# One stored value instead of a high and a low part for the mixers' results

## The chip, the cores and the metric

The kernel runs on one core of a Trainium2 chip. The metric is the device time of one launch in microseconds (us), the median of several runs. One execution was recorded by the hardware profiler. TensorE (PE) multiplies matrices and loads weights (PEld); VectorE (DVE), ScalarE (ACT) and GpSimd (POOL) work on tiles in on-chip memory (SBUF) and on PE's accumulators (PSUM banks). Each of them carries out its own instructions strictly in order. DMA transfers move data between DRAM and SBUF; they are issued by SyncE's queue (SP) or by POOL's.

## The reference: one hybrid layer

1152 tokens (1024 of a new stream, 8 times 16 of running streams) go through one layer of width 1024, all float32. What the change touches is the seam between the three mixers and the output projection:

```
xa, ga, z, xbc, dt, q, fpre, ig, og = split(rmsnorm(x) @ w_in)
ya = rglru(causal_conv(xa)) * gelu(ga)        # mixer A, 256 columns
yb = ssd_mixer(z, xbc, dt)                    # mixer B, 512 columns
yc = hgrn_mixer(q, fpre, ig, og)              # mixer C, 256 columns
x  = x + concat(ya, yb, yc) @ w_out           # output projection
x  = x + ffn(rmsnorm(x))                      # SwiGLU, then a last rmsnorm
```

## The kernel before

**Numbers.** Each float32 operand of a large product is split into a high part of type fp32r and a low part, the remainder. One product is then three matmuls, high·high, high·low and low·high (`mm3`, lines 142 to 147). A split is an ACT copy that rounds (line 180) and a subtraction (line 181), on DVE or POOL.

**Tiles.** The tokens are 9 tiles of 128, in 3 chunks of 3 tiles (384 tokens). Activations are held transposed: 128 channels on the partitions, tokens along the free axis. A chunk of the mixers' results is 8 blocks of 128 channels: blocks 0 and 1 come from mixer A, 2 to 5 from mixer B, 6 and 7 from mixer C.

**Stages.** First norm; input projections; mixer C for each token tile (`mix_c`, line 495); mixer A for each of its two channel blocks, all tokens at once (`mix_a`, line 350); the projections for B (`proj_xbc`, `proj_z`); then chunk by chunk mixer B for each tile (`mix_b`, line 686), the chunk's load (`mixt`, line 802) and the output projection with residual (`w_out`, line 812); then the feed-forward part, from about 600 us to the end.

**The buffer in DRAM.** `mixd` (line 111) holds the high and the low part of each value. `mix_a` makes them in two tiles `yh` and `yl` (line 391; the subtraction is POOL's) and issues 8 writes per block on SP. `mix_c` makes them from PSUM in the tile `mo`, with two ACT copies (line 631) and two DVE subtractions (line 632) per token tile, and issues two writes. `mix_b` does likewise in one of its work tiles (`ws` or `wb`, line 795) for the first two token tiles of a chunk; the third is split straight into the chunk's tile `mT` (line 793). `mixt` loads a chunk from `mixd` into `mT` with six transfers on POOL's queue: four of 2 blocks (384 KB) and two of 4 blocks for two token tiles (512 KB), all high parts and low parts alternating by blocks.

**Where mT lies.** `slot` (line 227) gives `mT` of chunk 0 the place of the last chunk's normed input, `mT` of chunk 1 the place that holds `s0f`, mixer B's states of the 8 running streams, which must first be computed and written out, and `mT` of chunk 2 the place of `ws`, mixer B's second set of work tiles.

**Order.** A scheduler in the framework places instructions per engine by priorities and by its own model of time. `feed()` (line 150) raises the priority of weight loads, their splits and evictions by 3000; `mix_b` is raised by 2000. `S` tiles (line 345 on: `rawxa`, `xa`, `g`, `yh`, ...) share six buffers of 128x1152 float32. `pw` is the PSUM bank of an output projection, `xr` its result with the residual, `wr_o`, `wh_o`, `wl_o` the raw, high and low weights of it, `pmb` and `pmc` the banks in which B's and C's results are transposed.

Of the kernel before, what the change touches and what calls it, by code (L numbers as in the profile page):

```python
# [11 lines left out]
F32 = mybir.dt.float32  # L12
F32R = mybir.dt.float32r
BF16 = mybir.dt.bfloat16
U8 = mybir.dt.uint8
AF = mybir.ActivationFunctionType
ALU = mybir.AluOpType

P = 128
D = 1024  # L20
KD = 8
NCHUNK = 3
TPC = 3
CH = TPC * P
# [66 lines left out]
def hybrid_step(ctx, tc, xT, xTp, vec, rows, nrow, wch, wtk0, wtk1, wout, wgate, wup, wdown,  # L91
# [3 lines left out]
    V, S, G, T = nc.vector, nc.scalar, nc.gpsimd, nc.tensor  # L95
    dma = nc.sync.dma_start
# [6 lines left out]
    dp = ctx.enter_context(tc.tile_pool(name="dp", bufs=1, space=bass.MemoryType.DRAM))  # L103
# [4 lines left out]
    zd = dp.tile([NT, P, 512], F32, tag="zd", name="zd")  # L108
    vod = dp.tile([NT, P, 512], F32, tag="vod", name="vod")
    qkbd = dp.tile([NT, P, 8 * P], F32, tag="qkbd", name="qkbd")  # L110
    mixd = dp.tile([NCHUNK, P, 2, KD, CH], F32, tag="mixd", name="mixd")
    ad = dp.tile([72, P], F32, tag="acd", name="acd")

    p1 = tc.tile_pool(name="p1", bufs=1)
# [24 lines left out]
    def mm(out, lhsT, rhs, start=True, stop=True):  # L139
        T.matmul(out, lhsT, rhs, start=start, stop=stop)  # L140
# [8 lines left out]
    def feed():  # L149
        return tc.high_priority(offset=PRI)  # L150
# [28 lines left out]
    def split(dst_hi, dst_lo, src, eng):  # L179
        S.activation(dst_hi, src, AF.Copy)  # L180
        eng.tensor_tensor(dst_lo, src, dst_hi.bitcast(F32), ALU.subtract)  # L181

    pr = p1.__enter__()
# [5 lines left out]
    hnw = pr.tile([P, 2], F32, name="hnw")  # L189
# [37 lines left out]
    def slot(c, name, dt=F32R):  # L227
        return xp.tile([P, 2, KD, CH], dt, tag=f"hT{c}", name=name)
# [79 lines left out]
    def stile(name, dt=F32):  # L308
        return pr.tile([P, NTOK], dt, tag="S", name=name, bufs=SB)
# [40 lines left out]
    def mix_a(j):  # L350
        x = conv_tile(j, j, [vc[:, V_CWA + i * 2 + j:V_CWA + i * 2 + j + 1] for i in range(4)],
                      vc[:, V_CBA + j:V_CBA + j + 1], f"xa{j}")
        ga = plain_tile(2 + j, f"ga{j}")

        t1, t2 = stile(f"a1_{j}"), stile(f"a2_{j}")
        for g, dst in ((0, t1), (1, t2)):
            for c in range(NCHUNK):
                cs = slice(c * CH, (c + 1) * CH)
                pb = bank("a", f"pa{j}{g}{c}", [CH])
                mm(pb, wbd[:, g * 2 + j, :], x[:, cs])  # L360
                S.activation(dst[:, cs], pb, AF.Tanh, bias=hb[:, g * 2 + j:g * 2 + j + 1], scale=0.5)
        t4, t3 = stile(f"a4_{j}"), stile(f"a3_{j}")
        S.activation(t4, t1, AF.Exp, bias=sp2[:, 2 + j:3 + j], scale=sp2[:, 2 + j:3 + j])
        S.activation(t1, t1, AF.Tanh, bias=sp2[:, j:j + 1], scale=sp2[:, j:j + 1])
        V.scalar_tensor_tensor(t2, t2, 1.0, x, ALU.add, ALU.mult)
        S.activation(t4, t4, AF.Identity, bias=cst[:, 1:2], scale=0.5)
        V.scalar_tensor_tensor(t3, t1, 1.0, t4, ALU.add, ALU.mult)
        V.scalar_tensor_tensor(t3, t3, 2.0, t4, ALU.subtract, ALU.mult)
        S.activation(t1, t1, AF.Sqrt)
        V.scalar_tensor_tensor(t1, t1, -1.0, t3, ALU.mult, ALU.mult)  # L370
        G.tensor_tensor(t2, t2, t1, ALU.mult)
        S.activation(t3, t3, AF.Identity, bias=cst[:, 3:4], scale=-2.0)
        sm = pr.tile([P, NB], F32, tag="sm", name=f"sm{j}")
# [12 lines left out]
        S.activation(t4, t4, AF.Identity, bias=ones[:, 0:1], scale=0.044715)
        G.tensor_tensor(t4, t4, ga, ALU.mult)
        S.activation(t4, t4, AF.Tanh, scale=float(np.sqrt(2.0 / np.pi)))
        V.scalar_tensor_tensor(t4, t4, 1.0, ga, ALU.add, ALU.mult)
        V.scalar_tensor_tensor(t4, t4, 0.5, t1, ALU.mult, ALU.mult)  # L390
        yh, yl = stile(f"yh{j}", F32R), stile(f"yl{j}", F32R)
        split(yh, yl, t4, G)
        for hl, v in enumerate((yh, yl)):
            for p, t, n in ((0, 1, 3), (3, 0, 1), (4, 4, 2), (6, 6, 3)):
                dma(mixd[p // TPC, :, hl, j, p % TPC * P:(p % TPC + n) * P], v[:, t * P:(t + n) * P].bitcast(F32))

# [96 lines left out]
    def mix_c(t):  # L495
# [12 lines left out]
        if not samp:  # L508
# [12 lines left out]
            for i in (1, 2, 3):  # L521
                n = 32 * i
# [53 lines left out]
        for h in range(4):  # L576
            j, r = h // 2, (h % 2) * 64
# [25 lines left out]
        else:  # L603
            pn = bank("c", f"pnc_{t}", [2, 64])
            for h in range(4):
                j, r = h // 2, (h % 2) * 64
# [18 lines left out]
        pm = bank("d", f"pmc{t}", [2, P])  # L625
        for j in range(2):
            T.transpose(pm[:, j, :], of[:, j * P:(j + 1) * P], ident)
        mo = pr.tile([P, 2, 2, P], F32R, tag="mo", name=f"mo{t}")
        for j in range(2):
            hn = hnw[:, j:j + 1]  # L630
            S.activation(mo[:, 0, j], pm[:, j, :], AF.Copy, scale=hn)
            V.scalar_tensor_tensor(mo[:, 1, j], pm[:, j, :], hn, mo[:, 0, j].bitcast(F32), ALU.mult, ALU.subtract)
        c, i = POS[t] // TPC, POS[t] % TPC
        for hl in range(2):
            dma(mixd[c, :, hl, 6:8, i * P:(i + 1) * P], mo[:, hl].bitcast(F32))
        if t == NT - 1:
            dma(o_psc, Sc)

# [47 lines left out]
    def mix_b(t, last):  # L686
        samp, first = t == 0, t == 1
        c, i = POS[t] // TPC, POS[t] % TPC
        dt, da, acs, tot, ex, tl = [sml[:, j, :] for j in range(6)]
        hc = slice(t * 8, t * 8 + 8)  # L690
        cs = slice(i * P, (i + 1) * P)
        bcount[0] += 1
        if bcount[0] % 2:
            wk6 = [pr.tile([P, 1024], F32, tag="S", name=f"wb{t}_{j}", bufs=SB) for j in range(6)]
        else:
            wk6 = [st["ws"][:, j, :] for j in range(6)]
# [91 lines left out]
        pm = bank("d", f"pmb{t}", [4, P])  # L788
        for k in range(4):
            T.transpose(pm[:, k, :], yf[:, k * P:(k + 1) * P], ident)  # L790
        if last:
            mT = st["mT", c]
            split(mT[:, 0, 2:6, cs], mT[:, 1, 2:6, cs], pm, V)
        else:
            mo = wk6[5].bitcast(F32R).rearrange("p (a k s) -> p a k s", a=2, s=P)
            split(mo[:, 0], mo[:, 1], pm, V)
            for hl in range(2):
                dma(mixd[c, :, hl, 2:6, cs], mo[:, hl].bitcast(F32))
        if t == NT - 1:
            dma(o_psb, Sb)  # L800

    def mixt(c):
        mT = slot(2 - c, f"mT{c}")
        st["mT", c] = mT
        for hl in range(2):
            for ks in ((0, 2), (6, 8)):
                G.dma_start(mT[:, hl, ks[0]:ks[1], :], mixd[c, :, hl, ks[0]:ks[1], :])
        for hl in range(2):
            G.dma_start(mT[:, hl, 2:6, 0:2 * P], mixd[c, :, hl, 2:6, 0:2 * P])


    def w_out(c):
# [119 lines left out]
    for t in range(NT):  # L932
        mix_c(t)
# [531 lines left out]
```

## Time and profile before

| | |
|---|---|
| time, median of 3 runs | 1440.03 us (1437.41 to 1441.8) |
| profiled execution, device time | 1439.05 us |
| its span on the core | 1437.3 us |
| PE busy | 1362.8 us (95%) |
| DVE, ACT, POOL busy | 1048.0, 544.5, 523.1 us (73%, 38%, 36%) |
| moved by DMA | 194.78 MB, 136 GB/s |

Busy time is the sum of an engine's instructions. With PE busy for 95% of the span, another engine's work costs time only where PE waits for it, or where PE runs at its lower clock. [...] The columns "idle before" tell what released an instruction that had waited.

### The profile page before, as it was taken

How to read it: one execution, taken by the hardware profiler on the slowest of the kernel's cores; microseconds unless marked ns; L12 is line 12 of the kernel's file. 1: busy time of each engine (PE TensorE's matmuls, PEld its weight loads, DVE VectorE, ACT ScalarE, POOL GpSimd, SP SyncE). 2: the span in 40 equal slices, each digit the busy share in tenths (PEclk: the TensorE clock that was granted, in tenths of full speed). 3: DMA queues.
4: the chain of work that ended last, by engine and by line, in shares of the span. 5: the costliest groups of instructions: out<-in, count | busy, mean ns of one | idle time of the engine just before them, and what ended most of it. 6: DMA issues, size and time to landing. Idle time of an engine off the chain costs nothing.

```text
span 1437.3 us, 24425 instructions
## 1 busy us (share of the span) xinstructions
PE 1362.8 (95%) x9383; PEld 1311.7 (91%) x9383; DVE 1048.0 (73%) x1923; ACT 544.5 (38%) x969; POOL 523.1 (36%) x417
## 2 busy tenths in 40 slices
PE   8998998999999999898999999999999999999986
PEld 7898887899998798798999999999999999989985
DVE  8475588878767575699556566565676688999896
ACT  7232276344455254465323222232222453333222
POOL 4160042211014420223554454544554533452453
PEclk9999999899999899898999999999999999999998
DMA  6264032433277877851422332222323263544523
GB/s 238 71 209 133 30 94 73 110 104 114 71 229 272 263 231 259 280 173 61 140 73 74 117 107 98 79 80 105 117 88 104 98 212 107 178 138 126 167 67 132
DMA packets 107001, 194.78 MB, mean 136 GB/s; under 512 B 10812, under 2 KB 66564, under 8 KB 106756
## 3 DMA queue, kind: packets, MB, share of 16 engines
q1 hardware_dynamic: 101988, 185.35, 39.7%
q0 software_dynamic: 4896, 7.87, 1.9%
q8 instruction: 74, 1.21, 0.4%
q14 instruction: 43, 0.35, 0.1%
HBM read 136.77 MB, written 56.41 MB: 134 GB/s over the span
## 4 chain that ended last, share of the span: by engine, by line
PE 37%; DVE 13%; DMA 6%; POOL 2%; issue 2%; ACT 1%; SPq 0%; DVEq 0%; POOLq 0%; ACTq 0%
PE pS_g L145 3%; PE pS_u L145 3%; PE pS_g L147 3%; PE pS_u L146 3%; PE pS_g L146 3%; PE pS_u L147 3%; PE pA_u L147 2%; PE pA_u L145 2%; PE pA_u L146 2%; PE pA_g L146 2%; PE pA_g L145 2%; PE pA_g L147 2%; PE pd L145 2%; PE pd L146 2%; PE pd L147 2%
## 5 line engine op out<-in xcount | busy, mean ns | idle before, releaser
L145 PE MATMUL pd<-e,as 128*128 128x256 f32 (+1 forms) x560 | 168.1, 302 | 8.2 <-ACT as L180 4.0
L146 PE MATMUL pd<-e,as 128*128 128x256 f32 (+1 forms) x560 | 166.0, 297 | 0.0
L147 PE MATMUL pd<-e,as 128*128 128x256 f32 (+1 forms) x560 | 163.0, 298 | 2.7 <-DVE as L181 2.6
L145 PEld LDWEIGHTS pd<-e,as 128*128 128x128 f32 x560 | 106.7, 191 | 11.7 <-ACT as L180 5.1
L181 POOL TENSOR_TENSOR al_u<-wr_u,ah_u 128x1024 fp32r<-128x1024 f32 x30 | 72.0, 2401 | 115.5 <-ACT ah_u L180 112.6
L147 PEld LDWEIGHTS pd<-e,as 128*128 128x128 f32 x560 | 105.9, 191 | 4.5 <-DVE as L181 4.3
L146 PEld LDWEIGHTS pd<-e,as 128*128 128x128 f32 x560 | 107.0, 191 | 0.1
L181 POOL TENSOR_TENSOR al_g<-wr_g,ah_g 128x1024 fp32r<-128x1024 f32 x30 | 72.0, 2400 | 93.9 <-ACT ah_g L180 93.2
L180 ACT ACTIVATE ah_g<-wr_g 128x1024 fp32r<-128x1024 f32 x30 | 31.7, 1060 | 142.6 <-PE pS_u L146 80.5
L1071 POOL TENSOR_TENSOR g<-g,pt_u 128x256 f32<-128x256 f32 (+1 forms) x80 | 77.0, 982 | 19.7 <-DVE pt_u L1067 15.4
L145 PE MATMUL pw<-mT,wh_o 128*128 128x384 f32 x192 | 68.1, 357 | 6.1 <-DMA mT<-mixd 4.0
L147 PE MATMUL pA_g<-b,al_g 128*128 128x256 f32 (+1 forms) x240 | 70.7, 295 | 1.1 <-POOL al_g L181 1.1
L145 PE MATMUL pS_g<-b,ah_g 128*128 128x256 f32 (+1 forms) x240 | 71.0, 296 | 0.4 <-ACT ah_g L180 0.4
L146 PE MATMUL pw<-mT,wh_o 128*128 128x384 f32 x192 | 67.9, 354 | 3.3 <-DMA mT<-mixd 3.3
L146 PE MATMUL pA_g<-b,ah_g 128*128 128x256 f32 (+1 forms) x240 | 71.0, 296 | 0.0
L145 PE MATMUL pA_u<-b,ah_u 128*128 128x256 f32 (+1 forms) x240 | 71.0, 296 | 0.0
L145 PE MATMUL pA_g<-b,ah_g 128*128 128x256 f32 (+1 forms) x240 | 70.8, 295 | 0.0
L147 PE MATMUL pA_u<-b,al_u 128*128 128x256 f32 (+1 forms) x240 | 70.8, 295 | 0.0
L146 PE MATMUL pA_u<-b,ah_u 128*128 128x256 f32 (+1 forms) x240 | 70.6, 294 | 0.0
L146 PE MATMUL pS_g<-b,ah_g 128*128 128x256 f32 (+1 forms) x240 | 70.6, 294 | 0.0
L145 PE MATMUL pS_u<-b,ah_u 128*128 128x320 f32 (+1 forms) x240 | 70.5, 295 | 0.0
L146 PE MATMUL pS_u<-b,ah_u 128*128 128x256 f32 (+1 forms) x240 | 70.3, 294 | 0.0
(699 smaller groups left out, 4783.7 us busy)
## 6 DMA issues: line engine op xcount, KB each, us to landing
wr_o<-in_dram SPq DMA_DIRECT2D x24, 512.0 KB, 4.7
wr_g<-in_dram SPq DMA_DIRECT2D x20, 512.0 KB, 3.5
wr_u<-in_dram SPq DMA_DIRECT2D x20, 512.0 KB, 3.5
wd<-in_dram SPq DMA_DIRECT2D x15, 512.0 KB, 4.1
wr_t<-in_dram SPq DMA_DIRECT2D x14, 512.0 KB, 3.5
ffd<-g SPq DMA_DIRECT2D x11, 640.0 KB, 3.9
fr<-ffd SPq DMA_DIRECT2D x11, 640.0 KB, 4.8
ffd<-g SPq DMA_DIRECT2D x11, 512.0 KB, 2.6
```

The lines of the kernel that those rows point to most:

```text
L145: T.matmul(out, ah, bh, start=start, stop=False)
L146: T.matmul(out, ah, bl, start=False, stop=False)
L147: T.matmul(out, al, bh, start=False, stop=stop)
L180: S.activation(dst_hi, src, AF.Copy)
L181: eng.tensor_tensor(dst_lo, src, dst_hi.bitcast(F32), ALU.subtract)
L1071: G.tensor_tensor(g, g, u, ALU.mult)
```

## The change

`mixd` becomes one float32 value per result, half its size. `mix_a` writes its product tile `g` itself (no `yh`, no `yl`, 4 writes per block for 8). `mix_c` has two ACT copies into a float32 tile `mo` with two buffers and one write; its DVE subtractions are gone. `mix_b` has one ACT copy and one write for a tile that goes through DRAM. `mixt` issues three transfers per chunk for six (two of 384 KB, one of 512 KB), each into the place of the low part; behind each it has, under `feed()`, an ACT copy into the high part and a DVE subtraction in place. Line numbers after it are lower by 3 to 6 from line 391 on (line 627 is 631 of before, 766 is 772, 770 is 776, 825 is 830); the new lines are 801 (transfer), 803 (copy) and 804 (subtraction).

```diff
-    mixd = dp.tile([NCHUNK, P, 2, KD, CH], F32, tag="mixd", name="mixd")
+    mixd = dp.tile([NCHUNK, P, KD, CH], F32, tag="mixd", name="mixd")
...
-        yh, yl = stile(f"yh{j}", F32R), stile(f"yl{j}", F32R)
-        split(yh, yl, t4, G)
-        for hl, v in enumerate((yh, yl)):
-            for p, t, n in ((0, 1, 3), (3, 0, 1), (4, 4, 2), (6, 6, 3)):
-                dma(mixd[p // TPC, :, hl, j, p % TPC * P:(p % TPC + n) * P], v[:, t * P:(t + n) * P].bitcast(F32))
+        for p, t, n in ((0, 1, 3), (3, 0, 1), (4, 4, 2), (6, 6, 3)):
+            dma(mixd[p // TPC, :, j, p % TPC * P:(p % TPC + n) * P], t4[:, t * P:(t + n) * P])
...
-        mo = pr.tile([P, 2, 2, P], F32R, tag="mo", name=f"mo{t}")
+        mo = pr.tile([P, 2, P], F32, tag="mo", name=f"mo{t}", bufs=2)
         for j in range(2):
-            hn = hnw[:, j:j + 1]
-            S.activation(mo[:, 0, j], pm[:, j, :], AF.Copy, scale=hn)
-            V.scalar_tensor_tensor(mo[:, 1, j], pm[:, j, :], hn, mo[:, 0, j].bitcast(F32), ALU.mult, ALU.subtract)
+            S.activation(mo[:, j], pm[:, j, :], AF.Copy, scale=hnw[:, j:j + 1])
...
-            mo = wk6[5].bitcast(F32R).rearrange("p (a k s) -> p a k s", a=2, s=P)
-            split(mo[:, 0], mo[:, 1], pm, V)
-            for hl in range(2):
-                dma(mixd[c, :, hl, 2:6, cs], mo[:, hl].bitcast(F32))
+            mo = wk6[5][:, 0:512].rearrange("p (k s) -> p k s", s=P)
+            S.activation(mo, pm, AF.Copy)
+            dma(mixd[c, :, 2:6, cs], mo)
...
-        for hl in range(2):
-            for ks in ((0, 2), (6, 8)):
-                G.dma_start(mT[:, hl, ks[0]:ks[1], :], mixd[c, :, hl, ks[0]:ks[1], :])
-        for hl in range(2):
-            G.dma_start(mT[:, hl, 2:6, 0:2 * P], mixd[c, :, hl, 2:6, 0:2 * P])
+        for ks, n in (((0, 2), CH), ((6, 8), CH), ((2, 6), 2 * P)):
+            hi, lo = [mT[:, hl, ks[0]:ks[1], 0:n] for hl in range(2)]
+            G.dma_start(lo.bitcast(F32), mixd[c, :, ks[0]:ks[1], 0:n])
+            with feed():
+                S.activation(hi, lo.bitcast(F32), AF.Copy)
+                V.tensor_tensor(lo, lo.bitcast(F32), hi.bitcast(F32), ALU.subtract)
```

The order of the instructions on POOL in chunk 0, where the first two chunks' loads stand (`ws` and `wb4` are work tiles of mixer B, `Sb` its running state), before:

```order
L807 DMA mT0_4406<-mixd_78 128x768 x4
L809 DMA mT0_4406<-mixd_78 128x4x256 x2
L775 TENSOR_TENSOR ws_4266<-ws_4266 128x512
L765 TENSOR_TENSOR Sb_296<-Sb_296,sml_315 128x512
L713 TENSOR_TENSOR ws_4266<-ws_4266,sml_315 128x512
L173 TENSOR_TENSOR ssb0_4609<-ssb0_4609,cst_82 128x2
L775 TENSOR_TENSOR wb4_3_4628<-wb4_3_4628,wb4_1_4626 128x512
L807 DMA mT1_4700<-mixd_78 128x768 x4
```

and now:

```order
L801 DMA mT0_4359<-mixd_78 128x768 x2
L801 DMA mT0_4359<-mixd_78 128x4x256
L769 TENSOR_TENSOR ws_4223<-ws_4223 128x512
L801 DMA mT1_4652<-mixd_78 128x768 x2
L759 TENSOR_TENSOR Sb_296<-Sb_296,sml_315 128x512
L769 TENSOR_TENSOR wb4_3_4582<-wb4_3_4582,wb4_1_4580 128x512
L759 TENSOR_TENSOR Sb_296<-Sb_296,sml_315 128x512
L707 TENSOR_TENSOR ws_4223<-ws_4223,sml_315 128x512
```

The load of chunk 1's first blocks now stands ahead of the two steps of `Sb` and of `wb4`'s addition; before, it stood behind the first and the addition.

The order on DVE in the last tile of mixer B and the end of chunk 1's output projection (`mT2` is the last chunk's tile, `pmb8` the bank from which its last third is split), before:

```order
L772 TENSOR_TENSOR wb8_1_5233<-pi8_5269,sml_315 128x256
L830 TENSOR_TENSOR xr1_6_5526<-xr1_6_5526,pw1_6_5534 128x384
L165 TENSOR_TENSOR wl_o12_5666<-wr_o12_5664,wh_o12_5665 128x1024
L225 TENSOR_TENSOR sq21_5307<-sq21_5307,tq21_6_5561 128x384
L776 TENSOR_TENSOR wb8_3_5235<-wb8_3_5235,py8_5277 128x512
L778 SCALAR_TENSOR_TENSOR wb8_3_5235<-wb8_3_5235,hr1_314,wb8_1_5233 128x512
L830 TENSOR_TENSOR xr1_6_5526<-xr1_6_5526,pw1_7_5570 128x384
```

and now:

```order
L766 TENSOR_TENSOR wb8_1_5187<-pi8_5223,sml_315 128x256
L804 TENSOR_TENSOR mT2_5176<-mT2_5176 128x768 x2
L770 TENSOR_TENSOR wb8_3_5189<-wb8_3_5189,py8_5231 128x512
L825 TENSOR_TENSOR xr1_6_5480<-xr1_6_5480,pw1_6_5488 128x384
L772 SCALAR_TENSOR_TENSOR wb8_3_5189<-wb8_3_5189,hr1_314,wb8_1_5187 128x512
L804 TENSOR_TENSOR mT2_5176<-mT2_5176 128x4x256
L165 TENSOR_TENSOR wl_o12_5620<-wr_o12_5618,wh_o12_5619 128x1024
L225 TENSOR_TENSOR sq21_5261<-sq21_5261,tq21_6_5515 128x384
```

The first two subtractions of the load stand between two steps of mixer B's last tile, ahead of line 770, and the third ahead of the next weights' low part.

## Rows read from the trace of the kernel before

**Rows 1.** The page: span, and each engine's busy time.

```profile
span 1437.3 us, 24425 instructions
...
PE 1362.8 (95%) x9383; PEld 1311.7 (91%) x9383; DVE 1048.0 (73%) x1923; ACT 544.5 (38%) x969; POOL 523.1 (36%) x417
```

**Rows 2.** Windows: length, busy of five engines, granted clock, DMA share, GB/s.

```profile
220.00:260.00 40.00, 37.83 (x203) 32.07 (x204) 32.61 (x65) 24.84 (x44) 8.83 (x10) 0.87 0.20 44
260.00:300.00 40.00, 36.47 (x211) 34.34 (x211) 31.16 (x70) 17.66 (x42) 8.58 (x13) 0.91 0.40 128
300.00:340.00 40.00, 40.00 (x246) 38.82 (x245) 32.66 (x70) 16.72 (x37) 4.83 (x13) 0.96 0.35 103
480.00:500.00 20.00, 18.97 (x83) 16.30 (x82) 11.51 (x20) 5.11 (x15) 9.72 (x12) 0.68 1.03 323
580.00:610.00 30.00, 22.98 (x113) 21.68 (x113) 17.12 (x26) 9.83 (x19) 7.81 (x9) 0.83 0.80 260
```

**Rows 3.** Timeline, mixer A's first block: start, length, what, idle before.

```profile
212.27 1.16 ACT L180 ACTIVATE yh<-g 128x1152 fp32r<-128x1152 f32 x1 [0.79 <-DVE g L390]
...
213.34 1.61 ACT L344 ACTIVATE xa<-rawxa,vc 128x1024 f32<-128x1024 f32 x2
...
213.56 2.69 POOL L181 TENSOR_TENSOR yl<-g,yh 128x1152 fp32r<-128x1152 f32 x1 [3.42 <-issue]
...
214.60 3.00 DVE L346 SCALAR_TENSOR_TENSOR xa<-rawxa,vc,xa 128x1024 f32<-128x1024 f32 x2 [1.23 <-ACT xa L344]
...
218.80 1.52 DVE L346 SCALAR_TENSOR_TENSOR xa<-rawxa,vc,xa 128x1024 f32<-128x1024 f32 x2
...
221.83 0.43 PE L140 MATMUL po<-vo,attc 128*128 128x64 f32 x2 [2.65 <-DVE attc L549]
```

**Rows 4.** Timeline, mixer A's second block.

```profile
260.21 2.68 POOL L181 TENSOR_TENSOR yl<-g,yh 128x1152 fp32r<-128x1152 f32 x1 [4.04 <-ACT yh L180]
...
261.89 2.35 DVE L346 SCALAR_TENSOR_TENSOR b<-rawb,vc,b 128x1024 f32<-128x1024 f32 x2 [1.24 <-ACT b L344]
...
266.57 0.41 PE L627 MATMUL pmc<-cio,oc 128*128 128x128 f32 x2 [1.62 <-DVE oc L624]
```

**Rows 5.** Mixer C's tile: its subtractions, duration min, median, max.

```profile
L632 DVE SCALAR_TENSOR_TENSOR mo<-pmc,hnw,mo x18: 335/344/348, 190.7 to 420.1; 128x128 fp32r<-128x128 f32 x18
```

**Rows 6.** Lines by shape: busy, mean ns of one, idle before.

```profile
L165 DVE TENSOR_TENSOR wl_o<-wr_o,wh_o 128x1024 fp32r<-128x1024 f32 x24 | 31.5, 1312 | 12.2 <-ACT wh_o L161 12.2
...
L161 ACT ACTIVATE wh_o<-wr_o 128x1024 fp32r<-128x1024 f32 x24 | 25.2, 1051 | 16.2 <-PE pw L146 12.1 <-PE ptz L147 2.2 <-DMA wr_o<-in_dram 1.9
```

**Rows 7.** The states' tile in 481 to 486: last write out, its landing.

```profile
L753 SPq DMA_DIRECT2D out_dram<-s0f x2: 338/338/338, 481.3 to 485.3; - x2
...
DMA to landing us min/median/max: 8.4/8.4/8.4
```

**Rows 8.** Timeline, the load of chunk 0.

```profile
481.54 0.98 PE L145 MATMUL pw<-mT,wh_o 128*128 128x384 f32 x2 [1.03 <-DMA mT<-mixd]
...
490.02 1.12 POOL L765 TENSOR_TENSOR Sb<-Sb,sml 128x512 f32<-128x512 f32 x1 [2.96 <-PE pi L140]
```

**Rows 9.** Timeline, the load of chunk 2.

```profile
581.06 2.25 POOL L807 DMA_DIRECT2D mT<-mixd  x4 [2.92 <-ACT tq L224]
...
584.78 2.13 POOL L775 TENSOR_TENSOR wb<-wb,wb 128x512 f32<-128x512 f32 x1
...
587.25 0.67 DVE L776 TENSOR_TENSOR wb<-wb,py 128x512 f32<-128x512 f32 x1
...
589.31 0.45 PE L146 MATMUL pw<-mT,wh_o 128*128 128x384 f32 x1 [1.94 <-DMA mT<-mixd]
...
596.00 0.98 PE L145 MATMUL pw<-mT,wh_o 128*128 128x384 f32 x2 [3.01 <-DMA mT<-mixd]
...
599.39 0.69 PE L146 MATMUL pw<-mT,wh_o 128*128 128x384 f32 x1 [1.34 <-DMA mT<-mixd]
```

**Rows 10.** The chain that ended last, around that load.

```profile
584.01 15.33 DMA mT<-mixd
```

More of the change, by code (lines that the diff above doesn't have):

```diff
@@ L627, in mix_c @@
             T.transpose(pm[:, j, :], of[:, j * P:(j + 1) * P], ident)
-        mo = pr.tile([P, 2, 2, P], F32R, tag="mo", name=f"mo{t}")
+        mo = pr.tile([P, 2, P], F32, tag="mo", name=f"mo{t}", bufs=2)
         for j in range(2):
-            hn = hnw[:, j:j + 1]
-            S.activation(mo[:, 0, j], pm[:, j, :], AF.Copy, scale=hn)
-            V.scalar_tensor_tensor(mo[:, 1, j], pm[:, j, :], hn, mo[:, 0, j].bitcast(F32), ALU.mult, ALU.subtract)
+            S.activation(mo[:, j], pm[:, j, :], AF.Copy, scale=hnw[:, j:j + 1])
         c, i = POS[t] // TPC, POS[t] % TPC
-        for hl in range(2):
-            dma(mixd[c, :, hl, 6:8, i * P:(i + 1) * P], mo[:, hl].bitcast(F32))
+        dma(mixd[c, :, 6:8, i * P:(i + 1) * P], mo)
         if t == NT - 1:
@@ L804, in mixt @@
         st["mT", c] = mT
-        for hl in range(2):
-            for ks in ((0, 2), (6, 8)):
-                G.dma_start(mT[:, hl, ks[0]:ks[1], :], mixd[c, :, hl, ks[0]:ks[1], :])
-        for hl in range(2):
-            G.dma_start(mT[:, hl, 2:6, 0:2 * P], mixd[c, :, hl, 2:6, 0:2 * P])
+        for ks, n in (((0, 2), CH), ((6, 8), CH), ((2, 6), 2 * P)):
[4 more added lines that the diff above has]
+                V.tensor_tensor(lo, lo.bitcast(F32), hi.bitcast(F32), ALU.subtract)
     def w_out(c):
```

## The prediction

> **What bounds the kernel now.** I read the page first: PE is busy 1362.8 of 1437.3 us and DVE 1048.0, so only some 74 us are not PE's, and what DVE, ACT and POOL save counts just where PE waits for it [rows 1]. So I went stage by stage with windows. From 300 to 340 us PE is busy all 40.00 us: nothing taken from another engine shortens that stretch. From 220 to 260 and from 260 to 300 it lacks 2.2 and 3.5 us and its clock is granted at 0.87 and 0.91; from 480 to 500 the clock is at 0.68, and from 580 to 610 it lacks 7.0 us at 0.83 with the DMA engines at 0.80 [rows 2]. These are the two places that the change touches with PE not covered: mixer A and C around 210 to 300, and the loads of the mixers' results. Third, the timeline there, for who releases whom. At mixer A, ACT's copy `yh` (1.16 us) stands right ahead of the convolution's first tap, DVE waits 1.23 us for that, then its two taps take 3.00 us while POOL makes `yl` for 2.69 us; the same pair takes 1.52 us at 218.80 without it. PE waits 2.65 us for DVE at 221.83 [rows 3]. In the second block it is 1.24 us of waiting, 2.35 us for the pair, and a wait of 1.62 us on PE [rows 4]. Last the chain that ended last: around 590 it is 15.33 us of the load of chunk 2 [rows 10], with three waits of PE on it, 1.94, 3.01 and 1.34 us [rows 9].
>
> **The change part by part.**
>
> *Mixer A.* Two ACT copies and two POOL subtractions go, and with them what they do to DVE. First block: the wait of 1.23 us, since the tap has no copy ahead of it (it is 213.34 less 212.27, about 1.1 us, that ACT is ahead), and 3.00 − 1.52 = 1.48 us of the pair [rows 3]. Second block: 1.24 us, and 2.35 − 1.52 = 0.83 us [rows 3, 4]. Together 2.71 + 2.07 = 4.8 us on DVE, which PE waits for in both blocks (2.65 and 1.62 us directly, further waits on DVE behind these). I count −4.8. If the gap goes, the clock should sag less: the shortfall is 40 × 0.13 + 40 × 0.09 = 8.8 us [rows 2]; I take a quarter, −2.2, because other waits in these 80 us stay. Bounds of the two together: −4.8 − 8.8 = −13.6, and upward +3.5, if the new order only shifts the stalls to other places and adds PE's whole present shortfall in the second window once more. The eight writes that go are of SP's queue, which PE waits for nowhere here: 0.
>
> [...]
>
> *Mixer C and B.* 18 DVE subtractions of 0.344 us go [rows 5], 6.2 us, and six of mixer B, estimated at 0.67 us from a DVE operation of the same 128x512 shape [rows 9], 4.0 us. Together 10.2 us of DVE, and half of the writes. I value this at 0: PE is the one that is full there (40.00 of 40) [rows 2]. If the steps were on the path where PE waits, perhaps −2; without PE's cover they would be worth the 10.2.
>
> *The load of chunk 2.* Six issues keep POOL from 581.06 to 584.78, when mixer B's addition `wb` may start, and the last piece lands near 599.4 [rows 9, 10]. Three issues of half the bytes take about half: POOL is free near 582.9, 1.9 us earlier, and the last piece lands near 584 + 15.33 / 2 − 2 = about 590. That removes up to all three waits, 1.94 + 3.01 + 1.34 = 6.3 us. Against it: each piece now needs a copy and a subtraction. Priced by the weights' split, 1.051 us on ACT and 1.312 on DVE per 128x1024, both inputs in SBUF [rows 6], a piece of 128x768 costs 0.79 and 0.98. And by the order on DVE two of the new subtractions stand ahead of mixer B's line 770, which at line 776 of before started at 587.25 [rows 9]. The second piece would land near 587, its split ends near 587 + 0.79 + 0.98 = 588.8 or a little later; so the last tile of mixer B is 2 us later there, and its result, the last third of `mT2`, is needed by the same matmuls. What is won by landing early is mostly lost by that: I take −1, bounds −6 (all waits gone) and +4 (2 us more for each of the two tile results that DVE's queue holds up: the load's split and mixer B's).
>
> *The loads of chunks 0 and 1.* There PE waits 1.03 us for the load now [rows 8]; otherwise mixer B's work covers it. A copy and a subtraction come behind each first piece, 0.79 + 0.98 = 1.77 us [rows 6], in two chunks 3.5; less the 1.03 that the halved load may win, +2.5. Bounds: −1 (the wait goes, mixer B covers the splits) and +9: the 3.5 and, as in the first rival, 5.1 more.
>
> **The sum.** −4.8 − 2.2 + 0 − 1 + 2.5 = −5.5. Against the profiled execution, 1439.05 us (its span of 1437.3 [rows 1] and 1.75 around it), that is 1433.5; the median of the runs shown is 1.0 us above the profiled execution, so on its scale 1434.5 us.
>
> **The rivals.** *Slower: the load of chunk 1 holds up POOL.* By the order on POOL its first pieces now stand ahead of `Sb` and `wb4`'s addition. They must wait until the place of `s0f` is free, so until its last write, issued at 485.3, has landed 8.4 us later [rows 7], at 493.7; with two issues of some 0.56 us (2.25 / 4) [rows 9], `Sb` starts at 495 where it started at 490.02 [rows 8]. Price +5.1 at a place where the clock is already at 0.68 [rows 2], and the copies of `mT1` hold ACT and DVE in the same way. It decides if mixer B's work on `Sb` is not hidden by other matmuls: then, with the gain at mixer A only in its first block (−2.7), chunk 2 at 0 and +2.5 as above, 1440.0 + 4.9 = 1445. Against it: the scheduler may have other matmuls in stock there, and what is lost early may come back when mixer B waits for DVE anyway.
>
> *No change: all is hidden.* The saved 4.8 us of DVE only turn into other waits of PE (it lacks 2.2 and 3.5 us in these windows, but for a dozen reasons), and the loads' gain and cost are both covered: 1440 within 3, so 1440. For it: PE's 95% [rows 1].
>
> *The new subtractions cost more than priced.* The removed ones read PSUM or one tile; the nine new ones take both inputs from SBUF, as the taps that stretched by 1.48 us beside POOL [rows 3]. If two of each chunk's three fall on a POOL operation that reads SBUF at half of that, it is 6 × 0.74 = 4.4, of which some 3 in view: 1437.5. [...]
>
> *The larger gain.* The clock comes back by more: −4.8 and half of 8.8, −4.4, with chunk 2 at −3 and the other loads at +1, −11.2: 1428.8.
>
> **How the numbers follow.** Chances: the forecast 0.34, the slower rival 0.28, no change 0.18, the costlier subtractions 0.08, the larger gain 0.12. About 0.3%, 4.3 us, is what a measurement of this kernel can tell from no change: faster is below 1435.7, slower above 1444.3. The forecast, with its own range of 1430 to 1438, is below 1435.7 for two thirds of its chance (0.24), the larger gain whole (0.12), and 0.05 come from the next two: 0.41. The slower rival, 1441 to 1451, is above 1444.3 for 0.23, and 0.04 come from the others: 0.27. The rest, 0.32, is no change. The range goes from 1426, which takes in the larger gain but for its lower end, to 1448, which takes in the slower rival but for its upper end; the bounds of the terms (−13.6 + 0 − 6 − 1, and +3.5 + 4 + 9) lie outside.
>
> **What would show it.** Mixer A is right if in the changed profile the taps' pair in both blocks takes about 1.5 us, ACT's copy is not ahead of them, and PE's windows from 220 to 300 have a higher busy share and clock; wrong, if PE idles as long there for other lines. Mixer C and B: PE full between 300 and 340 as before. Chunk 2: the load's end near 590, line 770 later than 587 (counted from the start of the stage), and PE's waits between 1 and 6 us in all, now for DVE. Chunks 0 and 1: the wait of `Sb` on POOL, and what follows in PE's waits between 480 and 500. The forecast fails if the loss there is over 5 us, if the time gained up to 400 us is under 3, or if a stage that the change doesn't touch, the feed-forward part, moves by more than 2.

## The result, and the profile after

The changed kernel takes 1423.32 us (median of 4 runs, 1419.54 to 1426.31) against 1440.91 us of the kernel before beside it: a ratio of 0.9893, 95% interval 0.9868 to 0.9917. It is 17.6 us faster where 5.5 were forecast, and outside the stated range. The page of its profiled execution, span and busy times, to be held against [rows 1]:

```profile
span 1417.7 us, 24313 instructions
...
PE 1352.8 (95%) x9383; PEld 1306.4 (92%) x9383; DVE 1047.2 (74%) x1908; ACT 550.1 (39%) x976; POOL 511.5 (36%) x406
```

DVE is as busy as before (1047.2 for 1048.0): the nine new subtractions take back what the 24 old ones left. POOL is busy 11.6 us less, and PE 10.0 us less with the same 9383 matmuls. PE's clock tells why: the profile gives the clock granted to PE as a share of full speed, and the trace lists it in stretches at 1.00 or at 0.5, 89.6 us at 0.5 before and 69.6 us after. By the granted share half of each is lost, so 44.8 and 34.8 us; from one start to the next, the output projection's matmuls of 128x384 at line 145 take 0.320 us at 0.5 and 0.175 us at 1.00, the median in both kernels. PE's gaps, from the span's start to its last matmul, fall from 62.1 to 53.0 us. 10.0 + 9.2 = 19.2 of the 19.6 us between the spans: by this reckoning half is PE's waiting, half its lower clock.

The same windows as in [rows 2] (length, busy PE, PEld, DVE, ACT, POOL, granted clock, DMA share, GB/s):

```profile
220.00:260.00 40.00, 36.02 (x199) 32.44 (x198) 29.74 (x56) 23.98 (x45) 8.32 (x12) 0.89 0.26 74
260.00:300.00 40.00, 39.64 (x246) 37.92 (x246) 31.38 (x68) 17.51 (x37) 4.86 (x11) 0.98 0.35 104
300.00:340.00 40.00, 40.00 (x254) 38.90 (x253) 33.13 (x69) 17.86 (x40) 4.04 (x11) 1.00 0.31 96
480.00:500.00 20.00, 20.00 (x132) 19.67 (x131) 16.77 (x30) 10.16 (x25) 7.92 (x7) 1.00 0.73 214
580.00:610.00 30.00, 27.27 (x138) 26.60 (x138) 23.96 (x31) 12.61 (x18) 6.50 (x3) 0.85 0.46 151
```

From 260 to 300 us PE is now busy 39.64 us for 36.47, at 0.98 for 0.91; from 480 to 500 the clock is whole, where it was 0.68, and the DMA engines stand at 0.73 for 1.03. The windows are not the same work in both kernels, though, since one is ahead. To compare progress, each matmul gets as its weight a typical undisturbed time, the 30th percentile of the times from one start to the next among the matmuls of its shape in the kernel before; the sum over matmuls started so far is the work done, and a kernel's lead at a time t of the kernel before is t less the time at which that kernel has done as much. Read so, the changed kernel is 3.6 us ahead at 200 us, and was so at 185, before anything that the change touches: that is how far two executions of the same instructions differ. At 400 us it is 12.4 ahead, at 700 us 19.4, and no more is gained in the feed-forward part (18.1 at 1150 us, 19.2 at 1400). So 8.8 us come between 200 and 400 us, with mixers A and C, and 7.0 between 400 and 700, with mixer B and the output projection.

**Mixers A and C.** The timeline of the changed kernel (start, length, engine, line, operation, idle before):

```profile
192.09 0.48 ACT L344 ACTIVATE xa<-rawxa,vc 128x128 f32<-128x128 f32 x1
...
203.21 1.24 ACT L344 ACTIVATE xa<-rawxa,vc 128x1024 f32<-128x1024 f32 x1 [1.03 <-DVE rawxa L338]
...
207.41 1.35 DVE L390 SCALAR_TENSOR_TENSOR g<-g,a 128x1152 f32<-128x1152 f32 x1
...
208.68 1.27 DVE L346 SCALAR_TENSOR_TENSOR xa<-rawxa,vc,xa 128x1024 f32<-128x1024 f32 x1
...
236.14 0.48 ACT L344 ACTIVATE b<-rawb,vc 128x128 f32<-128x128 f32 x1
...
248.56 1.24 ACT L344 ACTIVATE b<-rawb,vc 128x1024 f32<-128x1024 f32 x1 [2.29 <-DVE rawb L338]
```

From the kernel before (DVE and ACT):

```profile
205.84 0.55 DVE L338 TENSOR_TENSOR rawxa<-pmxa,rrow 128x384 f32<-128x384 f32 x1
...
211.06 0.42 ACT L538 ACTIVATE W<-W 128x256 f32<-128x256 f32 x1 [4.81 <-DVE W L537]
...
260.62 1.62 ACT L344 ACTIVATE b<-rawb,vc 128x1024 f32<-128x1024 f32 x2
```

In [rows 3] ACT's two pieces of the second block's convolution, `xa`, started at 213.34 us, right behind the copy `yh`, the large one first. Now the piece of 128 columns starts at 192.09 and the large one at 203.21, ahead of line 390, which ends the first block's gate. The large piece is 10.1 us earlier, 6.5 of them beyond the lead of 3.6 that was there before; the small one is 22 us earlier. The next convolution, `b`, started at 260.62 on ACT and now starts at 236.14 (small piece) and 248.56. That is far more than the 1.1 us of a copy that is gone. In the kernel before, the large piece's input was complete at 206.39 (205.84 + 0.55) and ACT then stood idle until 211.06, yet the piece started at 213.34; now it starts as soon as its input is there. So neither its input nor a busy ACT had held it. The trace does not say whether its tile was not free or whether it only stood behind `yh` in ACT's order; that is left to the experiments.

**The loads.** The new operations on `mT` (count, duration min, median, max in ns, first and last start), and the load's issues (count, KB each, median us from issue to landing), after and then before:

```profile
L803 ACT ACTIVATE mT<-mT x9: 842/845/1061, 466.4 to 570.4; 128x768 fp32r<-128x768 f32 x6, 128x1024 fp32r<-128x1024 f32 x3
L804 DVE TENSOR_TENSOR mT<-mT x9: 946/959/1886, 467.2 to 571.5; 128x768 fp32r<-128x768 f32 x6, 128x1024 fp32r<-128x1024 f32 x3
```

```profile
mT<-mixd POOLq DMA_DIRECT2D x6, 384.0 KB, 4.2
...
mT<-mixd POOLq DMA_DIRECT2D x3, 512.0 KB, 8.5
```

```profile
mT<-mixd POOLq DMA_DIRECT2D x12, 384.0 KB, 6.6
...
mT<-mixd POOLq DMA_DIRECT2D x6, 512.0 KB, 12.6
```

The copy of 128x768 takes 0.845 us and the subtraction 0.946 where 0.79 and 0.98 were forecast, and each landing takes a third less time. Around chunk 2:

```profile
560.54 1.92 POOL L801 DMA_DIRECT2D mT<-mixd  x3 [1.42 <-ACT wb L721]
...
565.07 1.27 POOL L769 TENSOR_TENSOR wb<-wb,wb 128x512 f32<-128x512 f32 x1 [2.61 <-issue]
565.27 2.75 DVE L804 TENSOR_TENSOR mT<-mT 128x768 fp32r<-128x768 f32 x2 [0.34 <-ACT mT L803]
...
567.95 0.68 DVE L770 TENSOR_TENSOR wb<-wb,py 128x512 f32<-128x512 f32 x1
...
571.50 1.23 DVE L804 TENSOR_TENSOR mT<-mT 128x1024 fp32r<-128x1024 f32 x1 [1.75 <-ACT mT L803]
...
579.24 1.01 PE L145 MATMUL pw<-mT,wh_o 128*128 128x384 f32 x2 [1.25 <-ACT mT L180]
```

Three issues, from 560.54 us, have landed by about 570.4, when the last copy starts: 10 us for the 18.3 of before [rows 9, 10]. The first of the two subtractions falls on POOL's addition (565.07 to 566.34) and takes 1.886 us, the largest of the nine; the next takes its 0.95. From its start to the end of the addition (565.27 to 566.34) it is 1.07 us, and it takes 1.886 − 0.946 = 0.94 us more than the next. It happens once in nine, so it costs about a microsecond. PE waits 2.20 and 1.25 us for `mT` in the whole run, the second for the third that mixer B splits straight into it, against 7.3 us before.

### The profile page after: what moved, and what is told of

The parts are those of the page before. It is cut to its first block, busy times and chain, and to the rows that moved or that the text cites. A ratio compares the mean times of both kernels' runs of the same rounds, so it can differ in the third digit from the quotient of the medians.

```text
span 1417.7 us, 24313 instructions
## 1 busy us (share of the span) xinstructions
PE 1352.8 (95%) x9383; PEld 1306.4 (92%) x9383; DVE 1047.2 (74%) x1908; ACT 550.1 (39%) x976; POOL 511.5 (36%) x406
## 4 chain that ended last, share of the span: by engine, by line
PE 64%; DVE 16%; DMA 8%; ACT 4%; issue 4%; POOL 2%; SPq 0%; DVEq 0%; POOLq 0%; ACTq 0%
PE pS_g L145 3%; PE pS_u L145 3%; PE pS_u L147 3%; PE pS_g L146 3%; PE pS_u L146 3%; PE pS_g L147 3%; PE pd L145 3%; PE pd L147 3%; PE pd L146 3%; PE pA_u L146 2%; PE pA_u L145 2%; PE pA_u L147 2%; PE pA_g L145 2%; PE pA_g L147 2%; PE pA_g L146 2%
## 5 line engine op out<-in xcount | busy, mean ns | idle before, releaser
L145 PEld LDWEIGHTS pd<-e,as 128*128 128x128 f32 x560 | 106.0, 190 | 12.3 <-ACT as L180 5.9
L147 PEld LDWEIGHTS pd<-e,as 128*128 128x128 f32 x560 | 104.5, 188 | 5.5 <-DVE as L181 5.5
L146 PEld LDWEIGHTS pd<-e,as 128*128 128x128 f32 x560 | 105.8, 189 | 0.0
L145 PE MATMUL pw<-mT,wh_o 128*128 128x384 f32 x192 | 68.7, 361 | 8.6 <-DVE xr L825 5.1
L145 PE MATMUL pmb<-hT,wh_b 128*128 128x384 f32 x192 | 67.6, 352 | 4.0 <-DVE rawb L338 3.0
```

Of the source, the lines that this page charges most:

```text
L145: T.matmul(out, ah, bh, start=start, stop=False)
L146: T.matmul(out, ah, bl, start=False, stop=False)
L147: T.matmul(out, al, bh, start=False, stop=stop)
```

## The experiments

Two theories of the first 8.8 us: W, the work of mixer A's split (copy on ACT, subtraction on POOL beside DVE); S, the buffers (`yh` and `yl` held two of the six S buffers that the convolution tiles use too). Of the other 7.0: traffic, DVE work, or the order of the instructions. All runs in one table; "200 to 400" and "400 to 700" are the change of the lead over the kernel before in that stretch, in us of one execution. Kernels with the same order of TensorE up to mixer B (the changed one, e6, e8, e9, n2, n4, n6) read 6.8 to 11.7 in the first, so about ±2.5 is what it can tell. The second is no better: the profiled execution lies between 3.8 us below the median of its kernel (the changed one) and 4.3 us above it (n5).

| run | median us | ratio to before (95%) | 200 to 400 | 400 to 700 |
|---|---|---|---|---|
| changed kernel | 1423.3 | 0.9893 (0.9868 to 0.9917) | +8.8 | +7.0 |
| e1 load alone | 1437.9 | 0.9999 (0.9984 to 1.0014) | +0.4 | −1.0 |
| e2 mixer A alone | 1436.8 | 0.9974 (0.9961 to 0.9987) | +12.0 | −7.0 |
| e3 mixer C alone | 1452.9 | 1.0098 (1.0082 to 1.0113) | −7.2 | −7.9 |
| e4 mixer B alone | 1443.6 | 1.0032 (1.0016 to 1.0048) | −0.1 | −8.1 |
| e5 before, split's work out | 1437.7 | 0.9995 (0.9979 to 1.0012) | +4.6 | −0.5 |
| e6 changed, split's work back | 1427.8 | 0.9926 (0.9903 to 0.9949) | +6.8 | +7.4 |
| e7 changed, buffers back | 1432.7 | 0.9957 (0.9936 to 0.9978) | +0.5 | +6.3 |
| e8 mixers A and C | 1431.3 | 0.9946 (0.9928 to 0.9965) | +10.0 | −2.8 |
| e9 changed, traffic back | 1436.5 | 0.9988 (0.9968 to 1.0009) | +6.9 | −8.1 |
| e10 changed, DVE work back | 1431.6 | 0.9949 (0.9928 to 0.9971) | +10.5 | −3.6 |
| e11 changed, one buffer less | 1430.0 | 0.9929 (0.9906 to 0.9952) | +9.5 | −0.6 |
| e12 before, one buffer less | 1439.2 | 1.0000 (0.9985 to 1.0015) | +6.6 | −9.0 |
| n1 before, multiplications swapped | 1441.0 | 1.0011 (0.9995 to 1.0026) | −2.8 | −1.0 |
| n2 changed, the same | 1426.5 | 0.9909 (0.9884 to 0.9934) | +11.7 | +5.7 |
| n3 before, transposes reversed | 1437.3 | 0.9990 (0.9974 to 1.0007) | +0.2 | +0.2 |
| n4 changed, the same | 1431.6 | 0.9944 (0.9924 to 0.9965) | +8.7 | −1.0 |
| n5 before, heads reordered | 1447.3 | 1.0046 (1.0031 to 1.0062) | +0.4 | −12.9 |
| n6 changed, loads swapped | 1434.5 | 0.9969 (0.9949 to 0.9989) | +10.1 | −2.9 |

### Parts alone (e1 to e4, e8)

e1: as the change in `mixt`, with every producer as before (exact copy and zero remainder):

```diff
+            G.dma_start(lo.bitcast(F32), mixd[c, :, 1, ks[0]:ks[1], 0:n])
+                S.activation(hi, lo.bitcast(F32), AF.Copy)
+                V.tensor_tensor(lo, lo.bitcast(F32), hi.bitcast(F32), ALU.subtract)
```

> Only the load is changed: one float32 value per result is loaded, and split behind the load; every mixer still makes two parts (an exact copy and a remainder of zero, the same instructions) and issues both writes. If the gain comes from the mixers' producers (theory P), this is within 4 us of the kernel before. If it comes from the halved load and its fewer issues on POOL's queue (theory L), it is 10 to 17 us faster, as the whole change.

Nothing moved (0.9999). A load of half the bytes and issues won nothing by itself, in the order that it got.

e2, e3, e4 and e8 take one mixer's lines (two in e8) of the change, and load its blocks once with a split behind; the other blocks stay in two parts:

```diff
+        one = [0]            # e2; [6] in e3, [2] in e4, [0, 6] in e8
+                if hl or ks[0] not in one:
                     G.dma_start(mT[:, hl, ks[0]:ks[1], :], mixd[c, :, hl, ks[0]:ks[1], :])
```

> Only mixer A's two blocks are kept as one value and split behind the load. Theory P: 6 to 10 us faster, most of it between 200 and 300 us, in half-clock time and in PE's waits for DVE. Theory L: a fourth of the load's gain, about 4 us faster, and that after 480 us.

> Only mixer C's two blocks are kept as one value (18 DVE subtractions of 0.34 us and 9 writes go). Theory P: 2 to 5 us faster, between 200 and 400 us. Theory L: about 4 us, after 480 us. The prediction valued this part at 0 to -2 us.

> Only mixer B's four blocks are kept as one value (6 DVE subtractions and 6 writes go, two issues of 512 KB become one in each chunk's load). Theory P: no change, within 3 us. Theory L: half of the load's bytes, about 8 us faster, after 480 us.

> Mixer A's and C's blocks as one value, mixer B's four blocks as two parts as before. The parts' own changes (A -2, C +14) would add to 1451 us. If the stretch up to 450 us depends on A and C alone, this is as far ahead there as the whole change (about 9 to 12 us), whatever the loads do after it: theory O (what follows 450 us depends on the order that comes out, not on the work) allows anything between 1420 and 1440 and then a gain or a loss of 5 to 15 us between 450 and 620.

Theory P (the mixers' producers) and theory L (the load) both fail on the totals: −2, +14 and +5 us for the parts against −17.6 for the whole. But the stretches sort it. Mixer A alone is 12.0 us ahead by 400 us, as much as the whole change, and with C 10.0: that part is A's. It then loses 7.0 behind 400 us; B and C alone lose 8 there, though each has less work and less traffic than the kernel before. Less work that costs 8 us points to something other than the work. Why C alone loses 7.2 us before 400 us, and with A nothing, was not settled; its order of TensorE is its own from 194.6 us on.

### Split's work or buffers (e5, e6, e7, e12, e11)

e5:

```diff
-        split(yh, yl, t4, G)
+        split(yh[:, 0:8], yl[:, 0:8], t4[:, 0:8], G)
```

> The kernel before, with mixer A's split cut down to 8 of 1152 columns, in the same two tiles yh and yl; their buffers are taken as before, and the product tile is written to both places in DRAM, so DMA volume stays (mixer A's low part is therefore wrong, it holds the full value). Theory W (the copy on ACT and the subtraction on POOL beside DVE's taps cost the time): some 10 us are won by 300 us of the span, as with mixer A's part alone. Theory S (yh and yl hold two of the six S buffers, so the next convolution tiles start late): nothing is won there, 0 to 3 us.

+4.6 us, between the two. It is not a clean test: the cut tiles are also given back earlier, by the 1.16 + 2.69 us of the split and since a 4 KB write, not eight large ones, must have landed. That alone does not explain it, since e7 below holds its tiles as briefly and reads +0.5; e5's order of TensorE is also another one. e6 and e7 are its halves done on the changed kernel:

```diff
+        S.activation(t4, t4, AF.Copy)                  # e6
+        G.tensor_tensor(t4, t4, t4, ALU.add)
...
+        yh, yl = stile(f"yh{j}", F32R), stile(f"yl{j}", F32R)      # e7
+        split(yh[:, 0:8], yl[:, 0:8], t4[:, 0:8], G)
+        for hl, v in enumerate((yh, yl)):
+            dma(scr[j, hl], v[:, 0:8].bitcast(F32))
```

> The changed kernel with the work of mixer A's split put back without its buffers: an ACT copy and a POOL addition of 128x1152 in place on the product tile (which is halved before and doubled by it, so the result is the same). Theory W: about 10 us slower than the changed kernel, 1433, lost between 200 and 300 us. Theory S: within 4 us of the changed kernel, 1420 to 1427.

> The changed kernel with the two S buffers of yh and yl taken again, each filled in 8 columns only and held until a small write of it (4 KB each) has landed. Theory W: within 4 us of the changed kernel, 1420 to 1427. Theory S: about 10 us slower, 1433, lost between 200 and 300 us.

The window from 200 to 400 us (columns as above; the count behind PE's busy time is its matmuls) for the kernel before, the changed one, e6 and e7:

```profile
200.00:400.00 200.00, 190.91 (x1164) 178.40 (x1163) 163.21 (x335) 93.43 (x191) 35.58 (x55) 0.94 0.33 97
```

```profile
200.00:400.00 200.00, 195.04 (x1245) 184.88 (x1244) 157.26 (x318) 96.80 (x201) 25.98 (x52) 0.97 0.34 104
```

```profile
200.00:400.00 200.00, 191.12 (x1221) 180.18 (x1220) 161.54 (x324) 96.78 (x194) 32.80 (x55) 0.97 0.33 95
```

```profile
200.00:400.00 200.00, 192.01 (x1176) 179.86 (x1177) 154.22 (x319) 93.44 (x194) 29.35 (x53) 0.94 0.32 93
```

With the work back PE starts 1221 matmuls there at a clock of 0.97; with the buffers back 1176 at 0.94, which is near the kernel before (1164, 0.94). The timelines say the same. In e6 `xa` starts as early as after the change, the lead of 3.6 us aside, though ACT has a copy and POOL an operation of 2.11 us again (here DVE's `qw` starts 0.18 us behind that operation and takes 2.21 us, for 0.42 at 258.78; the work costs some 2 us in all, 8.8 less 6.8, which is no more than this reading can tell):

```profile
195.75 0.47 ACT L344 ACTIVATE xa<-rawxa,vc 128x128 f32<-128x128 f32 x1
...
206.89 1.24 ACT L344 ACTIVATE xa<-rawxa,vc 128x1024 f32<-128x1024 f32 x1 [1.02 <-DVE rawxa L338]
...
213.71 2.11 POOL L392 TENSOR_TENSOR g<-g 128x1152 f32<-128x1152 f32 x1 [3.11 <-ACT g L391]
213.89 2.21 DVE L543 TENSOR_TENSOR qw<-W,ldq 128x256 f32<-128x256 f32 x1
```

In e7, where the copy `yh` is 8 columns wide, the pieces still start together, at 210.20, and the next convolution at 259.38, as before (213.34 and 260.62):

```profile
210.20 1.61 ACT L345 ACTIVATE xa<-rawxa,vc 128x1024 f32<-128x1024 f32 x2
...
259.38 1.61 ACT L345 ACTIVATE b<-rawb,vc 128x1024 f32<-128x1024 f32 x2
```

The stretch follows S: +6.8 with the work and without the buffers, +0.5 the other way round. The medians agree: e7 is 9.4 us slower than the changed kernel, with its interval of the ratio apart from that kernel's, and e6 is 4.5 slower, with intervals that overlap. All 9383 matmuls of e6 stand in the order of the changed kernel, so for TensorE this pair differs in the split's work alone; e7's order differs too. e12 and e11 go further: they free one more buffer, with no work and no transfer changed.

```diff
-        t4 = stile(f"g4_{j}")      # the gate is made in a4's tile
```

> The kernel before with the same edit and nothing else: no work and no transfer changed, one S buffer less in each of mixer A's blocks. Theory S: 3 to 7 us ahead at 400 us of the span. Theory W (the split's work): no lead there, within 2 us.

> The changed kernel with mixer A's gate tile g4 made in the buffer of a4, which is dead by then: one S buffer less per block, no work changed. If theory S holds (the S buffers held back what follows mixer A), a further 2 to 5 us are won between 200 and 300 us, 1418 to 1421. Without it: within 3 us, or slower, since the gate's steps now must wait for a4.

```profile
200.00:400.00 200.00, 191.11 (x1212) 179.92 (x1210) 167.99 (x340) 96.83 (x196) 35.13 (x56) 0.97 0.36 105
```

```profile
214.55 1.61 ACT L344 ACTIVATE xa<-rawxa,vc 128x1024 f32<-128x1024 f32 x2
...
255.10 1.61 ACT L344 ACTIVATE b<-rawb,vc 128x1024 f32<-128x1024 f32 x2
```

The kernel before, with this line alone, gains 6.6 us on itself by 400 us, with 1212 matmuls for 1164 in the window. Its `b` starts at 255.10 for 260.62, though its `xa` starts no earlier (214.55 for 213.34). That speaks for theory S with no split touched. The third freed buffer, in e11, gives nothing more that the measurement can tell (+9.5 for +8.8). And e12 ends at 1.0000, e11 6.7 us behind the changed kernel: what they win or keep before 400 us, they lose behind it.

One rival is left here. Freeing tiles also gives TensorE another order, and no run changes the order before 400 us with the tiles kept. Ten kernels in three orders without the two tiles (the changed kernel's; that of e2 and e10; e11's) read +6.8 to +12.0. The kernels with both tiles held read −2.8 to +0.4 in the old order, and −7.2 (e3), +4.6 (e5) and +0.5 (e7) in orders of their own. The two groups do not overlap, and `xa` starts between 192.1 and 196.4 us in the first and between 210.2 and 214.0 in the second; but the orders of the second group lie as far apart as the effect is large. So the freed tiles are the likely cause, and how much of the 8.8 us is only the draw of an order is not shown.

### Traffic, DVE work or order (e9, e10, n1 to n6)

e9 and e10:

```diff
+        for hl in (1, 0):                                           # e9: every write twice
+            dma(mixd[c, :, hl, 6:8, i * P:(i + 1) * P], mo)
+            G.dma_start(hi.bitcast(F32), mixd[c, :, 0, ks[0]:ks[1], 0:n])
...
+            V.scalar_tensor_tensor(mo2[:, 1, j], pm[:, j, :], hn, mo[:, j], ALU.mult, ALU.subtract)   # e10
```

> The changed kernel with its DMA traffic put back: every write of a mixer's result is made twice, into two planes, and each load too, the first into the high part's place, where the ACT copy overwrites it; so the bytes and the number of issues are as before, on POOL's queue too, and the engines' work is as after the change. If the stretch from 450 to 620 us (about 4 to 6 us won by the whole change) was won by the smaller traffic (theory T), these are lost: about 1428 to 1430, with the same lead at 450 us. If it was won by the work that mixers B and C no longer do on DVE (theory D), within 3 us of the changed kernel.

> The changed kernel with the 18 DVE subtractions of mixer C and the 6 of mixer B put back, their results left unused (mixer C's tile has one buffer again, as before). Theory D: 3 to 6 us slower than the changed kernel, lost in 200 to 410 and 450 to 620 us. Theory T: within 3 us of the changed kernel. The prediction valued this work at 0.

Both lose behind 400 us, by more than either theory gave (−8.1 and −3.6, where the changed kernel wins 7.0). Before 400 us the 18 subtractions of mixer C cost nothing that can be told (+10.5, in the order of e2, which has +12.0). But both also got another order from the scheduler. Compared instruction by instruction, from mixer B's first tile to the feed-forward part, TensorE's orders in the changed kernel and e6 are one and the same, e7's differs in five of 1317 matmuls, and these three win 6.3 to 7.4 us there; in e9 53% of the matmuls stand at the same place and in e10 25%. So the n runs change the order alone: two or more independent statements of mixer B written the other way round, all instructions and transfers kept.

```diff
-            for g in range(2):       # n1, n2: line 771
+            for g in (1, 0):
-        for k in range(4):           # n3, n4: line 789
+        for k in (3, 2, 1, 0):
-        for h in range(8):           # n5: the heads' products py
+        for h in (4, 5, 6, 7, 0, 1, 2, 3):
-        dma(wk6[0], xbcd[t])         # n6: moved behind zt's load
```

> The kernel before with two independent DVE multiplications of mixer B written in the other order: the same instructions, transfers and buffers; TensorE's order is as before up to mixer B's first tile and another one behind it. Theory O (what happens from 450 us on depends on the order that comes out): off by some 3 to 10 us in either direction from 450 to 700 us, so 1430 to 1448. Theory D (it depends on the work and the traffic): within 3 us of the kernel before.

> The changed kernel with the same two multiplications swapped; TensorE's order unchanged up to mixer B. The lead at 450 us stays at 7 to 10 us under both theories. Theory O: the 7.5 us that the changed kernel wins after 450 us shrink or vanish, 1423 to 1435. Theory D: they stay, 1420 to 1426.

> The kernel before with the four independent transposes at the end of a tile of mixer B in reverse order, else the same; the order behind it hardly moves. Theory O: 0 to 4 us off the kernel before, since the order is nearly the same. Theory D: within 3 us.

> The changed kernel with the same reversal; here TensorE's order moves in a fifth of its places between mixer B's first tile and the feed-forward part. Theory O: 1423 to 1435. Theory D: 1420 to 1426.

> The kernel before with the eight independent small products of mixer B's heads written in another order (4 to 7, then 0 to 3), else the same; TensorE's order as before up to mixer B, then another in an eighth of its places. Theory O: 3 to 10 us off the kernel before in either direction, after 450 us. Theory D: within 3 us.

> The changed kernel with two loads of mixer B's tile issued in the other order (z ahead of xbc), else the same; TensorE's order is unchanged up to mixer B and differs in half of its places behind it. Theory O: the lead at 450 us stays, what follows is anything between -10 and +8 us, 1420 to 1440. Theory D: 1420 to 1428.

The order alone moves the stretch from 400 to 700 us, in single executions by up to 13 us: the kernel before by −12.9 to +0.2, the changed one from +7.0 down to −2.9, with the whole work of the change in place. n5's profiled execution is 4.3 us slower than its median; by the ratios of whole runs n5's order costs the kernel before some 7 us (1.0046), and n6's takes 11 of the changed kernel's gain (0.9969 for 0.9893). In n5 the loss begins behind 425 us. What PE waits for between 425 and 630 us (total us, times, longest) there, and in the kernel before:

```profile
PE px L708 <- DMA wb<-xbcd: 4.3, 2, 3.9
...
PE pmb L790 <- DVE wb L786: 2.6, 1, 2.6
PE pmb L790 <- DVE wb L181: 2.4, 2, 1.7
```

```profile
PE px L708 <- DMA wb<-xbcd: 1.3, 1, 1.3
...
PE pmb L790 <- DVE wb L786: 0.7, 1, 0.7
```

The same load of `xbcd` is waited for 3 us longer, and the same steps of mixer B 2 to 4 us longer; only the order differs.

Is part of the 7.0 the lighter load's own? Seven kernels with the whole change won +7.0, +7.4, +6.3, +5.7, −0.6, −1.0 and −2.9 there, a mean of 3.1, though the first three are practically one order; five with the work of before stood at 0, −1.0, +0.2, −12.9 and −9.0, a mean of −4.5. The means differ in the direction of the lighter load; the values overlap (−2.9 against +0.2), and e1, the load alone in an order near the old one (78% of the matmuls at the same place), gained nothing. That stays open. What is shown is that orders of the changed kernel between 1423 and 1435 us are to be had with the same work.

## Why the prediction was wrong

Two steps failed: the cause given for mixer A's term, and the load's two terms, which carry the miss in time.

**Mixer A (−4.8, and −2.2 of the clock): near in size, by luck, and wrong in cause.** The step that failed is "Two ACT copies and two POOL subtractions go, and with them what they do to DVE". 8.8 us were won before 400 us where 7.0 were forecast, but not through that: with the work back the stretch still wins 6.8 (e6), and with the tiles back 0.5 (e7). The work is worth 2.0 us by the stretch and 4.5 by the medians, neither clear of noise. What had been put at nothing is what the two tiles do to the pool: there are six S buffers and nine tiles per block, and the next block's convolution needs a tile. Rows that could have hinted at it: the large piece of `xa` at 213.34 in [rows 3], behind the whole of the first block, with its input ready at 206.39 and ACT idle. I took that for a queue behind the copy, 1.1 us; it was 6.5 us beyond the lead. The trace before names no wait for a tile there. How much of the gain is the tiles' and how much the new order's stays open, as said above.

The 1.48 us that DVE's pair lost in the first block are near what was left of POOL's operation: its 2.69 us began 1.04 us before the pair [rows 3], so 1.65 were left. Nor did such stretching end with `yl`. In the changed kernel the first small tap starts 0.33 us behind POOL's line 387 and takes 2.50 us, where the third takes 0.33:

```profile
192.27 2.69 POOL L387 TENSOR_TENSOR g<-g,ga 128x1152 f32<-128x1152 f32 x1 [2.89 <-ACT g L386]
...
192.60 2.50 DVE L346 SCALAR_TENSOR_TENSOR xa<-rawxa,vc,xa 128x128 f32<-128x128 f32 x1 [0.17 <-ACT xa L344]
```

The rival of costlier subtractions (1437.5) fell: one of nine subtractions was stretched beside a POOL operation, by 0.94 us.

**Mixer C and B at 0:** nothing speaks against it before 400 us (e10, +10.5 with C's subtractions back); it is not testable behind it, where every such edit changes the order.

**Chunk 2 at −1 and chunks 0 and 1 at +2.5: here lies the miss.** As prices they were good: 0.845 and 0.946 us per piece for 0.79 and 0.98, the load landing in 10 us for 18, its issues taking POOL 1.92 us for 3.72 (581.06 to 584.78 [rows 9]), e1 at 0 for the whole load against a forecast of +1.5. As a forecast of the stretch they were 8.5 us off (−7.0 measured). They price the new steps at the places of the old kernel's rows. From the orders that I showed on POOL and DVE I read what stands ahead of what, and not that every row between 400 and 700 us comes from a new draw, which alone moves whole runs by 7 to 11 us. Whether the lighter load has a share of the 7.0 stays open.

**The slower rival** (the load of chunk 1 holds `Sb` by 5.1 us) fell. In the changed kernel:

```profile
467.26 1.01 PE L145 MATMUL pw<-mT,wh_o 128*128 128x384 f32 x2 [2.20 <-ACT mT L803]
...
477.66 1.09 POOL L801 DMA_DIRECT2D mT<-mixd  x2 [0.55 <-DMA out_dram<-s0f]
...
479.67 1.46 POOL L759 TENSOR_TENSOR Sb<-Sb,sml 128x512 f32<-128x512 f32 x1 [0.92 <-PE pi L140]
```

POOL waits 0.55 us for the states' write, where the rival has it wait the whole 8.4 of its landing, and `Sb` then waits for PE, 0.92 us. PE's first output projection waits 2.20 us for the copy, at the forecast price of 1.77 for copy and subtraction. **No change** fell: 17.6 us are clear of the noise. **The larger gain** (1428.8) came nearest in time. It rested on 4.4 us of the clock's return between 220 and 300 us, where the forecast had 2.2; the windows' shortfall went from 8.8 to 5.2 us (40 × 0.11 + 40 × 0.02), so 3.6 came back, in windows that are not the same work. It too said nothing of the tiles or the order.

**The rest.** 8.8 + 7.0 make 15.8 of the 19.6 us between the two profiled executions; 3.6 of the others were there at 200 us, before the change. The profiled execution of the changed kernel is the fastest of its four, 3.8 us below their median, so the two parts say less of the 17.6 us than their sum suggests.

## What to carry to other kernels

When an edit removes tiles, count the pool: how many tiles each iteration takes from it, how many buffers there are, and which later tile gets its buffer earlier; then look in the trace at where that tile's first instruction starts, and whether its input and its engine had been ready for it. That can outweigh the removed instructions (e7 against e6), and shows as work done earlier, not as a wait removed. Where a scheduler makes the order, measure its draw before crediting a stage: write two independent statements the other way round, in the old kernel and in the new one, and count as the edit's own only what is clear of that spread.

## What the runs showed of the hardware

In the profiled pair 10.0 of the 19.2 us are put down to stretches at a granted clock of 0.5 and 9.2 are PE's gaps, but the two do not always go together: in e6 PE's gaps are 60.9 us, near the 62.1 of the kernel before, and its stretches at 0.5 are 60.3 us against 89.6. That the clock sags less where PE's gaps go was the forecast's estimate from [rows 2]. DVE's `qw`, which started behind a POOL operation, ended 0.28 us after it in e6 (213.89 + 2.21 against 213.71 + 2.11), and the small tap of `xa` 0.14 us after one in the changed kernel (192.60 + 2.50 against 192.27 + 2.69). POOL and DVE started their instructions in the order of the lists under "The change": on POOL before line 775 at 485.80, 765 at 490.02, 775 at 493.10 and 807 at 494.32, and on DVE now the load's first two subtractions from 565.27, line 770 at 567.95 and the third subtraction at 571.50.
